# A Winograd-style convolution on one core: ten matmuls over zeros, one more casting load, one more store in halves

## The chip, the core and the metric

The kernel runs on one core of a Trainium2 chip. The core has a matrix engine (TensorE, PE in the profile, with its weight loads as PEld), VectorE (DVE), ScalarE (ACT), GpSimd (POOL) and SyncE (SP), and 16 DMA engines that move data between the device memory and the on-chip memory. The metric is the device time of one execution in microseconds; where several executions were timed, their median.

## The reference

The operation is a 3x3 convolution with a padding of one, over 16 images of 64 channels and 64x64 pixels, to 128 output channels, all in float32:

```python
batch, c_in, h, w, c_out = 16, 64, 64, 64, 128
x_pad = np.pad(x, ((0, 0), (0, 0), (1, 1), (1, 1)), mode='constant')
for kh in range(3):
    for kw in range(3):
        output[b, co] += weight[co, ci, kh, kw] * x_pad[b, ci, kh:kh+h, kw:kw+w]   # over all b, co, ci
```

The input is 16.8 MB, the output 33.6 MB.

## The kernel before, in words

Two images make a pair: 2 x 64 channels fill the 128 partitions. There are eight pairs, p = 0 to 7. In float16, the kernel computes two output rows j and j+1 at a time from three groups of products: U, from the sum of the two input rows in the middle (`ss`) with the weights' middle row G1; A, from single rows (`xs`) with G2-G1 and G0; B, from single rows with G0-G1 and G2. The even output rows are A + U, the odd ones B + U. Each group is a set of matmuls of 64 partitions by up to 512 columns, alternating between the two images of the pair, into two PSUM tiles (tag `acc`, 8 buffers).

Preparation: SP loads the weights (L42), pair 0 as float32 (`x0`, L45), and pairs 1 to 3 as float32 (`xf`, L49), all on one queue. POOL makes an identity and a float16 copy of the weights (L53). PE transposes the nine taps (L85, 18 small matmuls), ACT copies them out (L86), and POOL forms the differences G2-G1 and G0-G1 (L87, L88). POOL then issues `load(4)`: a DMA that reads float32 and writes float16 straight into an `xs` tile (L59). The `xs` pool has five buffers, so loads of pairs 5, 6 and 7 wait until an earlier pair's matmuls are done. Pair 0 is summed by DVE (L68) and cast by ACT (L92) in four pieces.

The main loop runs over the pairs. At its head POOL makes the row sums of the next pair (L68, two pieces) and, from p = 1 on, issues the load of pair p + 4. Then come four blocks of eight row pairs each. In a block PE computes U, ACT copies U out of PSUM (L155), PE computes A and DVE adds (L165), PE computes B and DVE adds (L168). For pairs that came in as float32 (`xf`), ACT also casts a quarter of the next pair twice in each of the blocks 2 and 3 (L160).

Stores: each pair has two output tiles of 2 MB, one per image (`ots`, tag `ot`, eight buffers, which the float32 inputs share). SP stores the first (L97 through `store`), ACT the second; the ACT store is held back until ACT has copied U of the next block (L161). A pair is stored whole after its last block, except pair 7, which is stored in two halves after blocks 1 and 3.

The order of each engine's instructions follows the program where `keep` marks them; the rest is placed by a scheduler, which also puts in the waits.

Of the kernel before, what the change touches and what calls it, by code (L numbers as in the profile page):

```python
# [8 lines left out]
F32 = mybir.dt.float32  # L9
F16 = mybir.dt.float16  # L10
# [3 lines left out]
def kernel(  # L14
# [6 lines left out]
    nc = tc.nc  # L21
    B, CI, H, W = x.shape
    CO = weight.shape[0]
    assert H == 64 and W == 64 and CI == 64 and CO == 128 and B % 2 == 0
    NP = B // 2
    RB = 8

    keep = tc.keep_in_program_order
# [4 lines left out]
    const = ctx.enter_context(tc.tile_pool(name="const", bufs=1))  # L33
    psum = ctx.enter_context(tc.tile_pool(name="psum", bufs=8, space=bass.MemoryType.PSUM))
    xpool = ctx.enter_context(tc.tile_pool(name="xpool", bufs=5))
# [8 lines left out]
    cuts = [(0, 18), (18, 34), (34, 50), (50, 64)]  # L44
    nc.sync.dma_start(x0, x_rows[0:128, :, :])  # L45
    xf = {}
    for p in (1, 2, 3):
        xf[p] = opool.tile([128, H, W], F32, tag="ot", name="xf")
        nc.sync.dma_start(xf[p], x_rows[128 * p : 128 * p + 128, :, :])  # L49
    ident = const.tile([128, 128], F16)  # L50
    make_identity(nc, ident)
    w16 = const.tile([CO, CI * 9], F16)
    keep(nc.gpsimd.tensor_copy(w16, w_raw))  # L53

    xs = {p: xpool.tile([128, H, W], F16, tag="xs", name="xs") for p in range(4)}

    def load(p):
        xs[p] = xpool.tile([128, H, W], F16, tag="xs", name="xs")
        keep(nc.gpsimd.dma_start(xs[p], x_rows[128 * p : 128 * p + 128, :, :]))  # L59
# [3 lines left out]
    def sums(eng, p, src, lo, n):  # L63
        if p not in ss:
            ss[p] = spool.tile([128, H // 2, W], F16, tag="ss", name="ss")
        v = src.rearrange("p (j i) c -> p j i c", i=2)
        keep(
            eng.tensor_add(  # L68
                ss[p][:, lo : lo + n, :], v[:, lo : lo + n, 0, :], v[:, lo : lo + n, 1, :]
            )  # L70
        )
# [5 lines left out]
    def wrow(i):  # L77
        return Wt[:, i, :, :].rearrange("p t c -> p (t c)")

    for kh, g in ((1, G1), (2, G2), (0, G0)):  # L80
        wp = psum.tile([128, 512], F32, tag="acc", name="wp")
        for k in range(3):
            t = 3 * kh + k
            for q in (0, 64):
                nc.tensor.matmul(wp[q : q + 64, k * CO : k * CO + CO], w16[:, t::9], ident)  # L85
        keep(nc.scalar.copy(wrow(g), wp[:, 0 : 3 * CO]))  # L86
    keep(nc.gpsimd.tensor_sub(wrow(G21), wrow(G2), wrow(G1)))  # L87
    keep(nc.gpsimd.tensor_sub(wrow(G01), wrow(G0), wrow(G1)))  # L88
    load(4)
    for n, (lo, hi) in enumerate(cuts):  # L90
        sums(nc.vector, 0, x0, RB * n, RB)
        keep(nc.scalar.copy(xs[0][:, lo:hi, :], x0[:, lo:hi, :]))  # L92
# [3 lines left out]
    def store(eng, p, b2, ot, lo, hi):  # L96
        return eng.dma_start(  # L97
            out_rows[2 * p + b2, :, lo:hi, :],
            ot.rearrange("p j i c -> p (j i) c")[:, lo:hi, :],
        )  # L100

    for p in range(NP):
        if p + 1 < NP:
            for lo in (0, 16):
                sums(nc.gpsimd, p + 1, xf.get(p + 1, xs[p + 1]), lo, 16)
        if p > 0 and p + 4 < NP:
            load(p + 4)
        ots = [
            opool.tile([128, H // 2, 2, W], F32, tag="ot", name="ot") for _ in range(2)
        ]  # L110
        for blk in range(4):
            j0 = blk * RB

            def group(wi_rows):

                tiles = [
                    psum.tile([128, RB, W], F32, tag="acc", name="acc") for _ in range(2)
                ]
                n = 3 * len(wi_rows)
                i = 0  # L120
                for wi, off in wi_rows:
                    for kw in (1, 0, 2):
                        c_lo, c_hi = max(0, 1 - kw), min(W, W + 1 - kw)
                        for b2 in range(2):
                            p0 = 64 * b2
                            lo, hi = j0, j0 + RB
                            if off is None:
                                rhs = ss[p][p0 : p0 + 64, lo:hi, c_lo + kw - 1 : c_hi + kw - 1]
                            else:
                                while 2 * lo + off < 0:  # L130
                                    lo += 1
                                while 2 * (hi - 1) + off > H - 1:
                                    hi -= 1
                                first = 2 * lo + off
                                last = 2 * (hi - 1) + off
                                rhs = xs[p][
                                    p0 : p0 + 64,
                                    first : last + 1 : 2,
                                    c_lo + kw - 1 : c_hi + kw - 1,
                                ]  # L140
                            nc.tensor.matmul(  # L141
                                tiles[b2][:, lo - j0 : hi - j0, c_lo:c_hi],
                                Wt[p0 : p0 + 64, wi, kw, :],
                                rhs,
                                start=i == 0,
                                stop=i == n - 1,
                            )
                        i += 1
                return tiles

            U = group([(G1, None)])
            us = []
            for b2 in range(2):
                ut = upool.tile([128, RB, W], F32, tag="ut", name="ut")
                keep(nc.scalar.copy(ut, U[b2]))  # L155
                us.append(ut)
            if p + 1 in xf:
                q = p + 1
                for lo in {2: (0, 16), 3: (32, 48)}.get(blk, ()):
                    keep(nc.scalar.copy(xs[q][:, lo : lo + 16, :], xf[q][:, lo : lo + 16, :]))  # L160
            while held:  # L161
                keep(store(nc.scalar, *held.pop(0)))
            A = group([(G21, 1), (G0, -1)])
            for b2 in range(2):
                nc.vector.tensor_add(ots[b2][:, j0 : j0 + RB, 0, :], A[b2], us[b2])  # L165
            Bt = group([(G01, 0), (G2, 2)])
            for b2 in range(2):
                nc.vector.tensor_add(ots[b2][:, j0 : j0 + RB, 1, :], Bt[b2], us[b2])  # L168
            parts = {3: (0, 64)} if p < NP - 1 else {1: (0, 32), 3: (32, 64)}
            if blk in parts:  # L170
                lo, hi = parts[blk]
                store(nc.sync, p, 0, ots[0], lo, hi)
                held.append((p, 1, ots[1], lo, hi))
# [32 lines left out]
```

## Time and profile before

| | before |
|---|---|
| time, median of 3 runs | 127.69 us (126.99 to 127.93) |
| the profiled execution's own time | 128.37 us |
| its span, first to last instruction | 126.6 us |
| PE busy | 105.8 us (84%) |
| DVE busy | 82.7 us (65%) |
| ACT busy | 52.0 us (41%) |
| POOL busy | 36.2 us (29%) |
| DMA packets | 46.57 MB written, mean 368 GB/s |
| device memory | 17.07 MB read, 33.55 MB written |

A line of the groups reads: source line, engine, operation, output <- inputs, shapes, count, then busy time, mean ns of one, and idle time before it with what ended it. A row of the stretches reads: from and to, length, busy us and count of PE, PEld, DVE, ACT and POOL, then the granted TensorE clock, the share of the 16 DMA engines' time in packets, and GB/s. Packets are counted in the stretch in which they start, so a share can pass 1. A casting load counts with the bytes that it writes, half of those that it reads. The issue of a DMA stands under the queue's name (SPq, ACTq, POOLq) or, for POOL, among its instructions; it says when the transfer was asked for, not when it moved.

### The profile page before, as it was taken

How to read it: one execution, taken by the hardware profiler on the slowest of the kernel's cores; microseconds unless marked ns; L12 is line 12 of the kernel's file. 1: busy time of each engine (PE TensorE's matmuls, PEld its weight loads, DVE VectorE, ACT ScalarE, POOL GpSimd, SP SyncE). 2: the span in 40 equal slices, each digit the busy share in tenths (PEclk: the TensorE clock that was granted, in tenths of full speed). 3: DMA queues.
4: the chain of work that ended last, by engine and by line, in shares of the span. 5: the costliest groups of instructions: out<-in, count | busy, mean ns of one | idle time of the engine just before them, and what ended most of it. 6: DMA issues, size and time to landing. Idle time of an engine off the chain costs nothing.

```text
span 126.6 us, 2416 instructions
## 1 busy us (share of the span) xinstructions
PE 105.8 (84%) x978; PEld 57.2 (45%) x978; DVE 82.7 (65%) x132; ACT 52.0 (41%) x84; POOL 36.2 (29%) x27
## 2 busy tenths in 40 slices
PE   0409999999999999999999999999999999990000
PEld 0304455555555555555555555555555555540000
DVE  0025777787778777877777778777877787774000
ACT  4329429933993399333333333333333333330000
POOL 2360093197996000940066000750000000000000
PEclk9999999999999999999999999999999999999855
DMA  6899999999999999999999999999999979999970
GB/s 171 352 456 394 295 306 363 430 440 430 391 324 290 362 396 334 347 321 375 368 352 362 303 409 419 430 419 425 435 430 425 399 316 425 414 438 414 417 324 21
DMA packets 3898, 46.57 MB, mean 368 GB/s; under 512 B 432, under 2 KB 432, under 8 KB 560
## 3 DMA queue, kind: packets, MB, share of 16 engines
q1 hardware_dynamic: 2016, 25.46, 48.2%
q10 hardware_dynamic: 1296, 16.78, 31.5%
q0 software_dynamic: 576, 4.19, 15.8%
q8 instruction: 7, 0.11, 0.3%
q14 instruction: 3, 0.02, 0.0%
HBM read 17.07 MB, written 33.55 MB: 400 GB/s over the span
## 4 chain that ended last, share of the span: by engine, by line
PE 82%; DMA 6%; DVE 2%; issue 1%; DVEq 0%; SPq 0%
PE acc L141 82%; DMA x<-in_x_dram 6%; DVE ot L165 1%; DVE ss L68 1%; DVE ot L168 0%; DVEq L201 0%; SPq L42 0%; DVEq L165 0%
## 5 line engine op out<-in xcount | busy, mean ns | idle before, releaser
L141 PE MATMUL acc<-xs,Wt 64*128 64x504 f16 (+3 forms) x768 | 88.8, 377 | 0.0
L141 PEld LDWEIGHTS <-Wt 64*128 64x128 f16 x960 | 56.1, 95 | 52.0 <-issue 6.0
L165 DVE TENSOR_TENSOR ot<-acc,ut 128x512 f32<-128x512 f32 x64 | 41.2, 686 | 23.8 <-PE acc L141 21.5
L155 ACT COPY ut<-acc 128x512 f32<-128x512 f32 x64 | 34.4, 589 | 54.3 <-issue 34.3
L168 DVE TENSOR_TENSOR ot<-acc,ut 128x512 f32<-128x512 f32 x64 | 41.1, 684 | 0.0
L141 PE MATMUL acc<-ss,Wt 64*128 64x504 f16 (+1 forms) x192 | 27.2, 384 | 3.9 <-DVE ss L68 3.9
L68 POOL TENSOR_TENSOR ss<-xs 128x1024 f16<-128x1024 f16 x8 | 16.8, 2127 | 20.4 <-DMA xs<-in_x_dram 20.4
L68 POOL TENSOR_TENSOR ss<-xf 128x1024 f16<-128x1024 f32 x6 | 14.0, 2355 | 12.5 <-DMA xf<-in_x_dram 12.5
L160 ACT CAST xs<-xf 128x1024 f16<-128x1024 f32 x12 | 12.0, 1057 | 0.0
L68 DVE TENSOR_TENSOR ss<-x 128x512 f16<-128x512 f32 x4 | 2.5, 685 | 8.8 <-DMA x<-in_x_dram 8.8
L59 POOL DMA_DIRECT2D xs<-in_x_dram x4 | 2.4, 601 | 10.4 <-ACT xs L160 10.4
L92 ACT CAST xs<-x 128x1024 f16<-128x1024 f32 (+2 forms) x4 | 3.9, 1042 | 2.6 <-DMA x<-in_x_dram 2.6
L85 PE MATMUL wp<-ident,w 128*64 128x128 f16 x18 | 1.3, 328 | 4.3 <-POOL w L53 4.3
L85 PEld LDWEIGHTS <-w 128*64 128x64 f16 x18 | 1.1, 209 | 4.3 <-POOL w L53 4.3
L86 ACT CAST Wt<-wp 128x384 f16<-128x384 f32 x3 | 1.2, 487 | 3.0 <-PE wp L85 3.0
L86 ACT ACT_TABLE_LOAD x1 | 1.3, 1283 | 0.7 <-PEq L190 0.7
L87 POOL TENSOR_TENSOR Wt<-Wt 128x384 f16<-128x384 f16 x1 | 0.9, 910 | 1.7 <-ACT Wt L86 1.7
L53 POOL CAST w<-w_raw 128x576 f16<-128x576 f32 x1 | 0.7, 664 | 2.3 <-DMA w_raw<-in_weight_dram 2.3
L88 POOL TENSOR_TENSOR Wt<-Wt 128x384 f16<-128x384 f16 x1 | 0.9, 910 | 0.0
masks.py:199 POOL TENSOR_SCALAR_AFFINE_SELECT ident<-ident 128x128 f16<-128x128 f16 x1 | 0.3, 294 | 0.1
masks.py:197 POOL MEMSET ident<- 128x128 f16 x1 | 0.2, 205 | 0.3 <-POOLq L190 0.3
L190 POOL MEMSET const-float32-0.0<- 128x1 f32 x1 | 0.1, 99 | 0.2 <-issue 0.2
(3 smaller groups left out, 0.3 us busy)
## 6 DMA issues: line engine op xcount, KB each, us to landing
out_dram<-ot SPq DMA_DIRECT2D x7, 2048.0 KB, 20.0
out_dram<-ot ACTq DMA_DIRECT2D x7, 2048.0 KB, 19.6
xf<-in_x_dram SPq DMA_DIRECT2D x3, 2048.0 KB, 22.6
xs<-in_x_dram POOLq DMA_DIRECT2D x4, 1024.0 KB, 24.2
x<-in_x_dram SPq DMA_DIRECT2D x1, 2048.0 KB, 7.6
out_dram<-ot SPq DMA_DIRECT2D x2, 1024.0 KB, 11.3
out_dram<-ot ACTq DMA_DIRECT2D x2, 1024.0 KB, 11.2
w_raw<-in_weight_dram SPq DMA_DIRECT2D x1, 288.0 KB, 2.8
```

Of the source, the lines that this page charges most:

```text
L59: keep(nc.gpsimd.dma_start(xs[p], x_rows[128 * p : 128 * p + 128, :, :]))
L68: eng.tensor_add(ss[p][:, lo : lo + n, :], v[:, lo : lo + n, 0, :], v[:, lo : lo + n, 1, :])
L85: nc.tensor.matmul(wp[q : q + 64, k * CO : k * CO + CO], w16[:, t::9], ident)
L86: keep(nc.scalar.copy(wrow(g), wp[:, 0 : 3 * CO]))
L87: keep(nc.gpsimd.tensor_sub(wrow(G21), wrow(G2), wrow(G1)))
L88: keep(nc.gpsimd.tensor_sub(wrow(G01), wrow(G0), wrow(G1)))
L92: keep(nc.scalar.copy(xs[0][:, lo:hi, :], x0[:, lo:hi, :]))
L141: nc.tensor.matmul(tiles[b2][:, lo - j0 : hi - j0, c_lo:c_hi], Wt[p0 : p0 + 64, wi, kw, :], rhs, start=i == 0, stop=i == n - 1,)
L155: keep(nc.scalar.copy(ut, U[b2]))
L160: keep(nc.scalar.copy(xs[q][:, lo : lo + 16, :], xf[q][:, lo : lo + 16, :]))
L165: nc.vector.tensor_add(ots[b2][:, j0 : j0 + RB, 0, :], A[b2], us[b2])
L168: nc.vector.tensor_add(ots[b2][:, j0 : j0 + RB, 1, :], Bt[b2], us[b2])
```

## The change

Three things are changed.

1. A tile of zeros is set by DVE, and ten matmuls over it (128 x 512, into a PSUM tile that nobody reads) are put on PE behind the transposes. The transposes get `keep`, so that PE's order is transposes, zeros, convolution.
2. Pair 3 is no longer loaded as float32 by SP and cast by ACT. It comes by a casting load on POOL, issued just before that of pair 4. `xs` is preset for three pairs instead of four, the fourth buffer going to `load(3)`. One buffer of the tag `ot` is no longer taken by an input.
3. Pair 6 is stored in halves, as pair 7 is.

```diff
-    for p in (1, 2, 3):
+    for p in (1, 2):
         xf[p] = opool.tile([128, H, W], F32, tag="ot", name="xf")
         nc.sync.dma_start(xf[p], x_rows[128 * p : 128 * p + 128, :, :])
+    zeros = const.tile([128, 512], F16)
+    keep(nc.vector.memset(zeros, 0.0))
+    warm = psum.tile([128, 512], F32, tag="acc", name="warm")
+
+    def spin(n):
+        for _ in range(n):
+            keep(nc.tensor.matmul(warm, zeros[:, 0:128], zeros))
+
...
-    xs = {p: xpool.tile([128, H, W], F16, tag="xs", name="xs") for p in range(4)}
+    xs = {p: xpool.tile([128, H, W], F16, tag="xs", name="xs") for p in range(3)}
...
             for q in (0, 64):
-                nc.tensor.matmul(wp[q : q + 64, k * CO : k * CO + CO], w16[:, t::9], ident)
+                keep(nc.tensor.matmul(wp[q : q + 64, k * CO : k * CO + CO], w16[:, t::9], ident))
         keep(nc.scalar.copy(wrow(g), wp[:, 0 : 3 * CO]))
+    spin(10)
     keep(nc.gpsimd.tensor_sub(wrow(G21), wrow(G2), wrow(G1)))
     keep(nc.gpsimd.tensor_sub(wrow(G01), wrow(G0), wrow(G1)))
-    load(4)
+    for p in (3, 4):
+        load(p)
...
-            parts = {3: (0, 64)} if p < NP - 1 else {1: (0, 32), 3: (32, 64)}
+            parts = {3: (0, 64)} if p < NP - 2 else {1: (0, 32), 3: (32, 64)}
```

In text and code pairs are numbered from 0: the fourth pair is p = 3, the seventh p = 6.

## The prediction

> **What bounds the kernel now.** I read the chain that ended last first, then the DMA queues, then the last stretches. The chain names PE; the question is whether that is the whole story.
>
> ```profile
> PE 82%; DMA 6%; DVE 2%; issue 1%; DVEq 0%; SPq 0%
> ...
> 9.55 103.26 PE acc L141 x948
> ...
> 114.78 0.33 SPq L97 DMA_DIRECT2D out_dram<-ot  x1
> 115.38 0.34 ACTq L97 DMA_DIRECT2D out_dram<-ot  x1
> ...
> SPq L201 <- DMA out_dram<-ot: 10.2, 5, 4.2
> ```
>
> PE works without a break from 9.55 to 112.81 us, but the span is 126.6. The last two stores are issued at 114.78 and 115.38, and SP then waits 10.2 us for stores at the kernel's end (L201). Those stores are 1 MB each; two of them at 426 GB/s take 4.9 us. The rest of the wait is a backlog: the end is set by DMA. The queues (packets, MB, share of the span on 16 engines) say how full it is:
>
> ```profile
> q1 hardware_dynamic: 2016, 25.46, 48.2%
> q10 hardware_dynamic: 1296, 16.78, 31.5%
> q0 software_dynamic: 576, 4.19, 15.8%
> q8 instruction: 7, 0.11, 0.3%
> ```
>
> They add up to 95.8%, 121.3 of 126.6 us. What is missing is seen in the stretches (the last two columns are DMA share and GB/s written):
>
> ```profile
> 80.00:98.00 18.00, 18.00 (x172) 9.75 (x168) 13.79 (x23) 5.90 (x12) 4.12 (x2) 1.00 1.01 428
> 98.00:100.00 2.00, 2.00 (x22) 1.04 (x18) 1.33 (x3) 1.07 (x2) 0.00 (x0) 1.00 1.02 434
> 100.00:102.00 2.00, 2.00 (x22) 1.16 (x20) 1.94 (x4) 0.10 (x1) 0.00 (x0) 1.00 0.67 279
> 102.00:104.00 2.00, 2.00 (x24) 1.09 (x20) 1.42 (x3) 0.97 (x2) 0.00 (x0) 1.00 0.75 320
> 104.00:106.00 2.00, 2.00 (x22) 1.10 (x20) 1.66 (x3) 0.93 (x2) 0.00 (x0) 1.00 1.14 483
> 106.00:120.00 14.00, 8.00 (x76) 4.08 (x71) 7.51 (x12) 2.29 (x5) 0.00 (x0) 0.97 0.99 419
> 120.00:122.00 2.00, 0.00 (x0) 0.00 (x0) 0.00 (x0) 0.00 (x0) 0.00 (x0) 0.50 1.01 426
> 122.00:124.00 2.00, 0.00 (x0) 0.00 (x0) 0.00 (x0) 0.00 (x0) 0.00 (x0) 0.50 0.32 135
> 124.00:126.00 2.00, 0.00 (x0) 0.00 (x0) 0.00 (x0) 0.00 (x0) 0.00 (x0) 0.50 0.04 16
> ```
>
> There are two thin places. One is a hole at 100 to 104 us: pair 5's stores have run out on most engines, and pair 6's are issued only at 101.97 (SP) and 102.58 (ACT). The other is a tail after 122 where only a few of the 16 engines still move data. The tail decides. Each transfer leaves 16 completion marks in the trace, which I read as one per DMA engine (sorted, us):
>
> ```
> pair 5, second store: 101.15 101.27 101.28 101.40 101.44 101.53 101.54 101.60 101.78 102.62 102.85 102.99 103.78 104.25 104.83 106.24
> last store:           122.76 122.78 122.79 122.79 122.80 122.81 122.81 122.82 122.83 122.84 122.88 123.10 123.58 123.78 124.73 125.61
> ```
>
> The slowest engine finished pair 5 at 106.24, long after pair 6's stores were there: it **never saw the hole**. From 106.24 to 125.61 it moved its sixteenth of the last 8.39 MB, 0.524 MB in 19.37 us = 27.1 GB/s, and 16 times that is 433, the full rate of the rows above. So the kernel ends when one late engine has done its share, and that engine is full from about 2 us on.
>
> **The change, part by part.**
>
> *Zeros and ten matmuls.* The memset of 128x512 f16 on DVE has no row; POOL's 128x128 memset took 0.205 us, so 0.2 to 0.8 us. DVE is idle until 8.80: cost nothing. The conv matmuls go in pairs of 64 rows; a spin fills 128 rows, so it should cost one pair's pace:
>
> ```profile
> 11.63 0.18 PEld L141 LDWEIGHTS <-Wt 64*128 64x128 f16 x2 [0.25 <-issue]
> 12.06 0.18 PEld L141 LDWEIGHTS <-Wt 64*128 64x128 f16 x2 [0.25 <-issue]
> 12.43 0.18 PEld L141 LDWEIGHTS <-Wt 64*128 64x128 f16 x2 [0.20 <-issue]
> 12.81 0.17 PEld L141 LDWEIGHTS <-Wt 64*128 64x128 f16 x2 [0.20 <-issue]
> 13.18 2.75 PEld L141 LDWEIGHTS <-Wt 64*128 64x128 f16 x26 [0.20 <-issue]
> ```
>
> A pair takes 0.43 us at first, 0.38 at the turn and 0.21 from 13.18 on, 3.6 us after PE began at 9.55; this is half pace, though the clock column reads 1.00 there. Nine pairs took 3.63 us and would take 1.9 at 0.21, so at most 1.7 us are to be had. The transposes end at 5.62 (4.31 + 1.31), so ten spins end between 7.7 and 9.9. The first conv matmul waits for DVE until 9.55: at worst 0.4 us late. PE then ends between 1.7 us earlier and 0.4 later. Neither moves the end: the last two stores are 4.9 us of work on the slowest engine, which so reaches them near 120.7, while they are issued by 115.4 plus 0.8 (from issue to rising rate at 101.97 to 102.75). PE has some 4 us of slack there. Gain taken: 0. `keep` on the transposes only fixes an order that the trace already shows.
>
> *Pair 3 by a casting load.* SP loses one 0.43 us issue, ACT four casts of 1.06 us, and two sums on POOL fall from 2.36 to 2.13 us: none on the path. POOL gains one issue of 0.57 to 0.70 us behind L88; queued behind it are the load of pair 4 and the sums of pair 1, for which POOL idles 7.23 us until 15.56. Pair 3 is needed near 48 us; a cast load issued at 7.63 landed by 23.05. SP's queue then has no pair 3 ahead of pair 0's stores. What counts is DMA time. Four casting loads took 15.8% = 20.0 us, 5.00 each; stores 31.5% = 39.9 us for 16.78 MB, 4.98 per 2.1 MB. By packets: 624 ns instead of 611, eight per engine, and plain packets beside casts also take 624: 0.1 + 0.1 us. **The unknown is what a cast does to the slowest engine.** Its lag behind the middle of the 16 is by such marks 1.5 us at 24.7, 2.4 at 30.5, 4.5 at 75.7 and 4.4 at 96.4, when the casts are over. Put on the four casts alone, that is 1.1 each. But there are seven instruction packets too (q8, 0.93 us each, one at 21.04 and then every 11 to 15 us), and the first cast load, beside other loads, left no lengthened packets before that one. Bounds: 0 to 1.1 us for the fifth; I take 0.2, nearer to that first stretch, since the added load runs there too. A gain is excluded, since as many bytes are read.
>
> Here the Trainium skill speaks against the change: "DMA: Bandwidth & Descriptors", section "Latency and other measured facts", has two of the 16 engines usually slower, with the descriptor rings of GpSimd's loads as a best guess. The trace has the late engine, not its number; by that rule the whole 1.1 us would fall due and the sum would be +1.45 us.
>
> *Pair 6 in halves.* SP and ACT each issue one store more (0.33 us). SP has only stores. On ACT the held store waits for DVE with the next copies behind it, as the page's waits show seven times now; ACT idles 54 us and PE's chain has no break there. The first halves come 12.8 us (a pair) before pair 7's 108.33, near 95.5 or 1.7 earlier, so the hole is filled. The packets become 8 KB: 309 ns each, 618 for 611, 16 times per engine = 0.1 us, and two more completions. Ten marks of pair 5 come before 102.75, so ten engines have something to gain, up to 1.9 us (the first falls idle at 100.83); the slowest has nothing: 0.
>
> A second rule of that page, section "Bandwidth", asks for large batches and gives a 1 MB load 78% of the peak. The row 120:122, when only 1 MB stores are left, has 426 GB/s; by the rule each of the four halves would take an estimated 0.6 us more (1.05 MB at 341 instead of 425 GB/s).
>
> **Sum.** 0.1 + 0.1 + 0.1 + 0.05 (completions) + 0.2 = +0.55 us on the span: 127.15. The profiled execution took 128.37, 1.77 around its span; it lies 0.68 above the median 127.69. Relative to the median: 128.2.
>
> **Rivals.**
> *The hole was the end's cause* (faster). If what I call one late engine is not one, but the work is passed on, the end follows the mean. The deficit is 0.94 us by GB/s (149 + 108 - 55, times 2 us, over 428) and up to 1.9 by the idle engines: 125.9 to 126.9 after the 0.15 of packets and completions, 126.4 in the middle. For it: ten engines did idle. Against it: the 19.37 us.
> *The fifth cast delays the late engine like the four before* (slower): 0.35 + 1.1 = +1.45 us, 129.1. It passes 1% from 0.93 us of added lag. For it: the lag grows from 20 to 77 us and not after. Against: the instruction packets, and the stretch of the new load.
> *The warm-up doesn't take*: zeros leave the pace at 0.43. PE ends at 113.2 at worst, inside its slack: 128.2 as well, no case of its own in time.
>
> **Chances.** Forecast: 0.52. Late engine made later: 0.26, all over 1% slower. Hole: 0.22, of which 0.13 over 1% faster and 0.09 within. Within 1% (126.4 to 129.0, about what a measurement of this kernel can tell from no change) that makes 0.61. The range takes in most of the hole's case and, above, 129.1 with 0.4 for a cast that costs more beside pair 0's stores than the average: 126.2 to 129.5.
>
> **What would show it.** Pairs at 0.21 us from the first conv matmul, PE's end near 111; no hole at 100 to 104; most completion marks of the last store near 121; its last mark still at 125 to 126.5. The lag of the last mark against the middle should grow from 2.8 to over 4 us, as the others get earlier. The prediction is wrong if the last mark comes with the others, or if the late engine's lag grows by a microsecond by 80 us.

## The result, and the profile after

The changed kernel takes 126.75 us (median of 22 runs, 126.31 to 127.87) against 127.94 us before (22 runs, 126.82 to 129.93, on the same chips): a ratio of 0.9928 with an interval of 0.9906 to 0.9949. It is faster by 0.7%, about 0.9 us. The ratios, here and below, take only the runs within 1.5% of the fastest of their kernel, the medians take all runs, so one doesn't follow from the other (by the medians the gain is 1.2 us). The forecast was 128.2 us, a little slower than before. The measured time lies in the range and in the bound of 1%, but the sign was wrong. The runs spread over 1.6 us after and over 3.1 us before: the one profile that the prediction was built on, 128.37 us, stood well above the median of its own kernel.

The page of the changed kernel, its queues (packets, MB, share of 16 engines):

```profile
q1 hardware_dynamic: 2016, 23.36, 44.6%
q10 hardware_dynamic: 1440, 16.78, 31.6%
q0 software_dynamic: 720, 5.24, 20.9%
q8 instruction: 7, 0.11, 0.3%
```

The chain that ended last (start, length, what):

```profile
5.64 3.89 PE warm L56 x10
9.53 101.53 PE acc L151 x919
```

The queues' shares add up to 97.4% of 125.0 us, 121.8 us; before it was 121.3. So the DMA engines are as loaded as before and idle less. PE ends at 111.06 instead of 112.81 us, as the zeros cost 3.89 us in a gap that was there. The weight loads show the pace (start, length; each line one spin or a group):

```profile
8.11 0.15 PEld L56 LDWEIGHTS <-zeros 128*128 128x128 f16 x1 [0.28 <-issue]
8.54 0.15 PEld L56 LDWEIGHTS <-zeros 128*128 128x128 f16 x1 [0.28 <-issue]
8.94 0.10 PEld L56 LDWEIGHTS <-zeros 128*128 128x128 f16 x1 [0.25 <-issue]
9.46 0.59 PEld L151 LDWEIGHTS <-Wt 64*128 64x128 f16 x8 [0.42 <-issue]
```

Spins go at 0.43 us until about 8.9; the trace's clock record has the full clock from 8.90 us on, before the first convolution matmul. In the kernel before it starts at 13.27. (The clock column of the stretches reads 1.00 ahead of that first entry, which is why it told nothing.)

The stretches of the changed kernel (the last two columns are DMA share and GB/s written):

```profile
24.00:26.00 2.00, 2.00 (x22) 1.05 (x20) 1.40 (x3) 0.42 (x1) 0.59 (x1) 1.00 1.14 205
26.00:28.00 2.00, 2.00 (x22) 1.06 (x20) 1.27 (x3) 1.07 (x2) 2.00 (x2) 1.00 0.96 143
...
100.00:102.00 2.00, 2.00 (x22) 1.03 (x20) 1.40 (x3) 1.07 (x2) 0.00 (x0) 1.00 1.00 418
102.00:104.00 2.00, 2.00 (x22) 1.08 (x20) 1.94 (x4) 0.64 (x2) 0.00 (x0) 1.00 0.98 414
...
120.00:122.00 2.00, 0.00 (x0) 0.00 (x0) 0.00 (x0) 0.00 (x0) 0.00 (x0) 0.50 0.86 365
122.00:124.00 2.00, 0.00 (x0) 0.00 (x0) 0.00 (x0) 0.00 (x0) 0.00 (x0) 0.50 0.21 86
```

The hole at 100 to 104 us is gone. New is a weak stretch at 24 to 28, where the kernel before has this row:

```profile
26.00:28.00 2.00, 2.00 (x23) 1.06 (x19) 1.70 (x3) 0.13 (x1) 2.00 (x2) 1.00 1.05 426
```

The engines count as busy, but move less. Almost only casting loads run there, so twice the written bytes count, and even then 143 is 286 GB/s. Of the casting loads' packets, which took 624 ns elsewhere, 24 of the 25 that start at 26 to 28 us took 0.7 to 1.56 us; I call this a spell. The completion marks of the changed kernel's last two stores show that the last engine is no longer 2.8 us behind the middle of its store, but 1.4:

```
last store on SP:  120.89 121.45 121.52 121.53 121.54 121.83 121.89 122.32 122.64 123.03 123.12 123.14 123.29 123.31 123.32 123.96
last store on ACT: 121.51 121.75 121.82 121.85 121.87 122.15 122.19 122.63 122.94 123.32 123.33 123.34 123.44 123.48 123.48 124.15
```

In these two executions the last mark went from 125.61 to 124.15 us, while the middle of the last store stayed (122.82 and 122.78). The question is which part made the most loaded engine earlier, and whether it is the same in other executions.

### The profile page after: what moved, and what is told of

Its sections match the earlier page's. It is cut to its first block, busy times and chain, and to the rows that moved or that the text cites. A ratio compares the mean times of both kernels' runs of the same rounds, so it can differ in the third digit from the quotient of the medians.

```text
span 125.0 us, 2436 instructions
## 1 busy us (share of the span) xinstructions
PE 108.1 (86%) x988; PEld 56.7 (45%) x988; DVE 82.8 (66%) x133; ACT 48.2 (39%) x80; POOL 36.4 (29%) x28
## 4 chain that ended last, share of the span: by engine, by line
PE 85%; DMA 2%; DVE 1%; issue 1%; POOL 1%; DVEq 0%
PE acc L151 81%; PE warm L56 3%; DMA w_raw<-in_weight_dram 2%; PE wp L93 1%; DVE ot L175 1%; POOL w L61 1%; DVEq L211 0%; DVE ot L178 0%; DVEq L175 0%
## 5 line engine op out<-in xcount | busy, mean ns | idle before, releaser
L151 PE MATMUL acc<-xs,Wt 64*128 64x504 f16 (+3 forms) x768 | 93.1, 373 | 0.0
L151 PEld LDWEIGHTS <-Wt 64*128 64x128 f16 x960 | 54.3, 94 | 48.6 <-issue 0.8
L151 PE MATMUL acc<-ss,Wt 64*128 64x504 f16 (+1 forms) x192 | 31.8, 377 | 0.0
L76 POOL TENSOR_TENSOR ss<-xs 128x1024 f16<-128x1024 f16 x10 | 21.0, 2126 | 21.7 <-DMA xs<-in_x_dram 11.1
L76 POOL TENSOR_TENSOR ss<-xf 128x1024 f16<-128x1024 f32 x4 | 9.4, 2364 | 11.8 <-DMA xf<-in_x_dram 11.8
L170 ACT CAST xs<-xf 128x1024 f16<-128x1024 f32 x8 | 8.0, 1058 | 0.0
L67 POOL DMA_DIRECT2D xs<-in_x_dram x5 | 2.9, 587 | 9.3 <-PE acc L151 9.3
L56 PE MATMUL warm<-zeros 128*128 128x512 f16 x10 | 4.0, 574 | 0.0
L56 PEld LDWEIGHTS <-zeros 128*128 128x128 f16 x10 | 1.3, 137 | 2.3 <-issue 2.2
## 6 DMA issues: line engine op xcount, KB each, us to landing
out_dram<-ot SPq DMA_DIRECT2D x4, 1024.0 KB, 13.2
out_dram<-ot ACTq DMA_DIRECT2D x4, 1024.0 KB, 12.8
```

The costliest lines, as they stand in the source:

```text
L56: keep(nc.tensor.matmul(warm, zeros[:, 0:128], zeros))
L76: eng.tensor_add(ss[p][:, lo : lo + n, :], v[:, lo : lo + n, 0, :], v[:, lo : lo + n, 1, :])
L151: nc.tensor.matmul(tiles[b2][:, lo - j0 : hi - j0, c_lo:c_hi], Wt[p0 : p0 + 64, wi, kw, :], rhs, start=i == 0, stop=i == n - 1,)
```

## Experiments

Each was timed in 12 runs (the one with eight short spins in 6) beside the kernel before on the same chip. For reading them side by side I use one table, made from the DMA records of each profiled execution: how many MB the 16 engines are behind a steady 0.4275 MB per us that starts at 2.5 us (a casting load counted by what it reads, instruction packets left out). 0.43 MB is 1 us of all engines. "Clock" is the first full-clock entry of the clock record.

| kernel | median us | ratio to before (interval) | clock full from | first store issued | behind at 24 | at 48 | at 100 | at 104 us | last mark |
|---|---|---|---|---|---|---|---|---|---|
| before, first profile | 127.69 | | 13.27 | 25.13 | 0.07 | 0.16 | 0.35 | 0.81 | 125.61 |
| before, again | 127.25 | 0.9968 (0.9914 to 1.0022) | 14.94 | 26.06 | 0.07 | 0.68 | 0.78 | 1.15 | 125.18 |
| whole change | 126.75 | 0.9928 (0.9906 to 0.9949) | 8.90 | 23.42 | -0.03 | 0.50 | 0.51 | 0.55 | 124.15 |
| halves alone | 127.75 | 1.0042 (0.9999 to 1.0084) | 15.03 | 25.97 | 0.03 | 0.68 | 0.76 | 0.77 | 125.26 |
| cast alone | 127.23 | 0.9996 (0.9959 to 1.0033) | 12.34 | 24.72 | 0.03 | 0.24 | 0.33 | 0.61 | 123.94 |
| zeros alone | 126.58 | 0.9945 (0.9911 to 0.9978) | 8.58 | 23.80 | 0.02 | 0.47 | 0.49 | 0.53 | 123.90 |
| zeros and halves | 127.13 | 0.9963 (0.9935 to 0.9991) | 10.05 | 23.82 | 0.01 | 0.53 | 0.53 | 0.57 | 124.22 |
| zeros and cast | 126.78 | 0.9951 (0.9920 to 0.9983) | 7.74 | 23.45 | 0.06 | 0.46 | 0.49 | 0.54 | 124.09 |
| cast and halves | 126.77 | 0.9977 (0.9941 to 1.0014) | 14.50 | 26.33 | 0.07 | 0.87 | 0.93 | 0.93 | 125.16 |
| zeros, 8 full spins late | 128.04 | 1.0041 (1.0015 to 1.0067) | 8.91 | 23.90 | 0.09 | 0.45 | 0.48 | 1.05 | 125.63 |
| zeros, 8 short spins late | 126.57 | 0.9889 (0.9845 to 0.9932) | 7.63 | 23.48 | 0.03 | 0.48 | 0.50 | 0.56 | 123.74 |
| zeros, pair 6's stores later | 126.67 | 0.9957 (0.9926 to 0.9988) | 10.12 | 23.78 | 0.01 | 0.49 | 0.51 | 0.81 | 124.00 |
| zeros, pair 0's stores later | 127.51 | 0.9996 (0.9958 to 1.0034) | 8.68 | 24.99 | 0.05 | 0.35 | 0.47 | 0.52 | 124.24 |
| whole, pair 0's stores later | 127.64 | 0.9994 (0.9954 to 1.0034) | 9.47 | 25.07 | 0.05 | 0.11 | 0.22 | 0.25 | 123.47 |
| pair 0 in halves alone | 127.58 | 1.0015 (0.9978 to 1.0052) | 14.68 | 19.35 | 0.12 | 0.32 | 0.40 | 1.15 | 125.36 |
| whole, pair 0 in halves | 127.34 | 0.9970 (0.9936 to 1.0003) | 8.12 | 17.71 | 0.18 | 0.44 | 0.46 | 0.49 | 124.04 |

A profile is one execution; the medians are of twelve runs (three in the first row, 22 for the whole change, six with eight short spins). The kernel before was profiled twice, and the two rows differ by 0.5 MB at 48 us.

### The kernel before, once more

No edit.

> The kernel before, unchanged, for a second profile. Theory A (a property of the program): the last store's 16 completion marks look as they did, fifteen within 2 us of the middle and the last one 2.8 us behind it, and the late mark is 4 to 5 us behind the middle from 75 us on. Theory B (a draw of the run): the late mark's lag differs by more than 1 us from one execution to the next, and the time with it. Time within 0.5% either way.

As to the lag, theory B held: here the last mark lies 1.5 us behind the middle of its store, not 2.8. In this execution the clock rose at 14.94 instead of 13.27 us, so more convolution matmuls went at half pace. This execution's weight loads around the rise:

```profile
14.23 0.17 PEld L141 LDWEIGHTS <-Wt 64*128 64x128 f16 x2 [0.25 <-issue]
14.65 0.17 PEld L141 LDWEIGHTS <-Wt 64*128 64x128 f16 x2 [0.25 <-issue]
15.01 0.97 PEld L141 LDWEIGHTS <-Wt 64*128 64x128 f16 x10 [0.18 <-issue]
```

PE's chain ended at 113.73 against 112.81. In the six profiles without zeros the clock rose at 12.34 to 15.03 us: a draw over 2.7 us, half of which PE loses.

Every run has its span and its mean granted clock on record, and this tells whether the time goes with that draw. In all 16 profiles the full clock lasts 102.40, 105.81 or 109.23 us, which is 30, 31 or 32 times 3.413. The mean counts the time ahead of the rise as full, so with the span it gives the moment of the fall and, but for a multiple of 3.413 us, that of the rise (worked out so for the 16 profiled runs, it meets the profile's own to within 0.13 us). Taken to lie between 12.0 and 15.4 us, it splits 134 timed executions of this kernel: the 39 with a rise before 12.75 have a median of 126.9 us, and 22 of them lie under 127; the 37 with a rise after 14.25 have 128.0, and none lies under 127. So the clock's draw moves the time, by about 1 us, but not alone: the 39 reach up to 128.2.

The early loss is a draw too, and comes as a spell at 34 to 44 us that the first profile hardly had. First the rows of the second profile, then those of the first:

```profile
34.00:36.00 2.00, 2.00 (x22) 1.05 (x18) 2.00 (x4) 1.72 (x3) 1.70 (x3) 1.00 0.93 270
42.00:44.00 2.00, 2.00 (x22) 1.09 (x20) 1.27 (x3) 1.03 (x2) 0.00 (x0) 1.00 0.95 258
```

```profile
34.00:36.00 2.00, 2.00 (x22) 1.07 (x20) 1.30 (x3) 1.72 (x4) 1.98 (x3) 1.00 1.01 352
42.00:44.00 2.00, 2.00 (x22) 1.04 (x18) 1.65 (x3) 0.11 (x1) 0.00 (x0) 1.00 0.99 348
```

The two executions end within 0.43 us of each other by different ways: the first has the middle of its last store at 122.82 and one engine 2.79 us behind, the second the middle at 123.73 and 1.45. The late engine of the prediction was real, but how late it is belongs to the execution, not to the program.

### One part of the change at a time

```diff
-            parts = {3: (0, 64)} if p < NP - 1 else {1: (0, 32), 3: (32, 64)}
+            parts = {3: (0, 64)} if p < NP - 2 else {1: (0, 32), 3: (32, 64)}
```

> Pair 6 in halves alone. Theory A (the late engine sets the end): the hole at 100 to 104 us is gone, the time is within 0.3 us of before, since the late engine never saw the hole. Theory C (the hole is the end's cause): 0.9 to 1.6 us faster.

The hole is gone (0.76 behind at 100 us, 0.77 at 104) and the time isn't better: 1.0042, with an interval that just touches 1. Theory C's 0.9 to 1.6 us faster is out, which speaks against the hole as the end's cause by itself. Theory A's 0.3 us holds by the medians (127.75 against 127.62 for the kernel before beside it); the ratio's middle is 0.5 us slower, and whether the halves cost something isn't settled.

```diff
-    for p in (1, 2, 3):
+    for p in (1, 2):
...
-    load(4)
+    for p in (3, 4):
+        load(p)
```

> Pair 3 by a casting load alone. Theory A with a lag that the casts make: 0.2 to 1.5 us slower. Theory A with a lag that the float32 load of pair 3 beside pair 0's stores makes: 0.5 to 1.5 us faster, and the late mark at 75 to 96 us less than 3 us behind the middle. Theory C: within 0.3 us.

0.9996: the casting load costs and brings nothing that 12 runs can tell. Neither of theory A's two forms got its size. The last mark lies 1.4 us behind its middle in this profile, with an early rise of the clock at 12.34 us; with one profile the two can't be parted.

```diff
+    zeros = const.tile([128, 512], F16)
+    keep(nc.vector.memset(zeros, 0.0))
+    warm = psum.tile([128, 512], F32, tag="acc", name="warm")
...
+    spin(10)
```

> The ten matmuls over zeros alone. PE's end is near 111.1 instead of 112.8 us. Theory A: the time is within 0.3 us, since PE has about 4 us of slack against the late engine. Theory C: the hole shrinks by what PE gains, 1.7 us, and the time falls by 0.9 to 1.6 us, as much as by the halves.

0.9945: the zeros alone make three quarters of the whole change's gain, and their interval takes in all of it. The 0.3 us that theory A allowed were passed (0.7 us at the ratio's middle). PE ended at 111.44 and the hole was gone, as theory C said; but theory C had also promised this to the halves, which didn't get it.

### Pairs of parts

Each leaves out one part of the whole change.

> Zeros and halves, pair 3 still as float32. The zeros alone leave no hole, so both theories H and E expect the time of the zeros alone, 0.4 to 0.8% under before; if the halves cost something of their own (alone they were at 1.004), 0.1 to 0.3% faster only.

> The whole change without the halves. Theories H and E: PE is early, no hole, 0.4 to 0.8% faster than before, the same as the whole change. If the halves are what the whole change has over the zeros, less than that.

> The whole change without the ten matmuls. PE's clock rises between 12 and 15.2 us, after the first convolution matmul. Theory H: no hole whatever PE does, so 0.4 to 0.8% faster than before. Theory E: the early loss stays a draw, time within 0.4% of before.

With zeros the ratios are 0.9963 and 0.9951, intervals below 1; without them 0.9977, an interval that takes in 1. The five kernels with zeros and no later delay, the whole change among them, look alike in the table: full clock by 10.05 us, first store at 23.4 to 23.8 us, 0.46 to 0.53 MB behind at 48 us, next to nothing lost after. Those without zeros scatter from 0.16 to 0.87 MB at 48 us. For cast and halves, theory H's figure (0.4 to 0.8% faster) is neither reached nor excluded. Its twelve runs fall into two groups, seven at 126.4 to 126.9 us and five at 127.7 to 128.2, and its profile (127.82 us) is of the second: without the zeros this kernel can be as fast as the whole change, but not in every run.

### The hole put back: eight more spins late

```diff
+        if p == 5:
+            spin(8, psum.tile([128, 512], F32, tag="acc", name="warm2"))
```

> The ten matmuls over zeros, and eight more ahead of pair 5 (about 1.7 us at 0.21 each), so that pairs 5 to 7 come as late as in the kernel before while all earlier stores come early. Theory H (an early PE helps because pair 6's stores then meet no hole): the hole at 100 to 104 us is back, and the 0.5% of the ten matmuls alone are lost, time within 0.3% of before. Theory E (it helps by what happens before 45 us: when the first stores meet the loads): 0.4 to 0.8% faster than before, as with the ten alone.

The gain is lost and more: 1.0041. The eight spins in PE's chain (start, length), and then the stretches of this kernel, which show the hole:

```profile
74.51 1.83 PE warm L56 x8
```

```profile
100.00:102.00 2.00, 2.00 (x22) 0.98 (x20) 1.27 (x3) 0.70 (x2) 0.00 (x0) 1.00 0.88 369
102.00:104.00 2.00, 2.00 (x24) 0.90 (x21) 1.44 (x3) 1.07 (x2) 0.00 (x0) 1.00 0.52 221
```

That looked like theory H. But the run brought an eighth instruction packet of 16 KB (at 115.93 us), and it made all of pairs 5 to 7 late. Two more runs look at these separately.

### The hole put back: only pair 6's stores later

ACT copies an idle tile twice and touches pair 6's first output tile before SP and ACT may store the pair. PE's instructions stay as they were.

```diff
+            while late:
+                for _ in range(2):
+                    keep(nc.scalar.copy(pad, pad))
+                o = late[0][2]
+                keep(nc.scalar.copy(o[:, 0, 0, 0:8], o[:, 0, 0, 0:8]))
+                keep(store(nc.sync, *late.pop(0)))
             while held:
...
+                if p == 6:
+                    late.append((p, 0, ots[0], lo, hi))
```

> The ten matmuls alone, but ACT does two idle copies and a touch of pair 6's first output tile before SP and ACT may store pair 6: these two stores come 1.5 to 2 us later, PE and its instruction count stay. Theory H (the zeros help because pair 6's stores meet no hole): the hole at 100 to 104 us is back and the time is 0.5 to 1.2 us over the ten matmuls alone, which puts it within 0.4% of before. Theory L (they help because less is left for the most loaded engine by 80 us, and what the eight extra matmuls cost was an eighth instruction packet): hole, but less than 0.4 us over the ten matmuls alone.

SP's store moved from 100.64 to 102.91 us, ACT's from 101.24 to 102.17. The stretches of this kernel:

```profile
100.00:102.00 2.00, 2.00 (x24) 0.92 (x20) 1.42 (x3) 1.46 (x3) 0.00 (x0) 1.00 0.86 360
102.00:104.00 2.00, 2.00 (x22) 0.92 (x20) 2.00 (x4) 1.19 (x4) 0.00 (x0) 1.00 0.83 344
```

A hole of 0.30 MB, 0.7 us of all engines, and the time stays: 126.67 us, ratio 0.9957. As to the hole, theory L held. Pair 6's stores were issued at 102.17 and 102.91, and about half of the marks of pair 5's stores come before 103 us: the hole fell to engines that were ahead. The last mark is at 124.00, as with the zeros alone.

### The same instructions without the delay

```diff
-            spin(8, psum.tile([128, 512], F32, tag="acc", name="warm2"))
+            for _ in range(8):
+                keep(nc.tensor.matmul(warm2[:, 0:8], zeros[:, 0:128], zeros[:, 0:8]))
```

> The ten matmuls, and ahead of pair 5 eight matmuls of 8 columns instead of 512: as many instructions as in the run with eight full ones, but some 0.5 us of PE instead of 1.7. If that run was slow by its eighth instruction packet near 116 us, this one has that packet too and is 0.7 to 1.3 us over the ten matmuls alone. If it was slow by PE's 1.7 us, this one is within 0.5 us of the ten alone.

The eight short matmuls in PE's chain:

```profile
74.10 0.29 PE warm L120 x8
```

The eighth instruction packet came (113.96 us), pair 6's first store went out at 100.91 us instead of 102.87 (0.4 us of that is a later start of the convolution in the profile with full spins), and the time is 126.57 instead of 128.04. So the packet by itself costs nothing. 1.5 us more of PE, from pair 5 on, cost 1.5 us, though the last stores still went out at 115.7 and 116.3 us; this goes directly against the prediction's "some 4 us of slack". Whether PE's lateness costs this by itself, or only together with the packet, isn't shown: a late PE from pair 5 on without an eighth packet wasn't run. In the run with full spins the marks of a store at 114 us lie within 0.8 us of each other; of the next, behind that packet at 115.93, the last mark is 2.0 us behind the middle.

### When the first stores start

The delay of pair 6's stores, moved to pair 0: the same edit with `p == 0`, on the zeros alone and on the whole change.

> The same delay on pair 0's stores instead, so that the first stores come at 25 us as in the kernel before while PE's clock is up from the start. Theory S (the spell of lengthened packets at 25 to 28 us comes when the first stores meet the loads at that moment): no spell or another place for it, the loss by 44 us under 0.2 MB instead of 0.42, up to 0.5 us faster than the ten matmuls alone. Theory P (it goes with PE's pace): spell unchanged, time unchanged within 0.3 us.

> The whole change with the same delay on pair 0's stores. Theory S: up to 0.5 us faster than the whole change, some 1% under before. Theory P: as the whole change, 0.5 to 0.9% under before.

The stretches of the zeros alone, and then of the same with pair 0's stores held back by 0.6 us (ACT) and 1.9 us (SP):

```profile
26.00:28.00 2.00, 2.00 (x22) 1.09 (x20) 1.48 (x3) 1.07 (x2) 2.00 (x2) 1.00 0.95 262
```

```profile
26.00:28.00 2.00, 2.00 (x22) 1.04 (x19) 1.27 (x3) 1.07 (x2) 2.00 (x2) 1.00 1.00 418
```

The spell at 25 to 28 us went, as theory S said; on the zeros alone a smaller one came at 40 to 48 us (0.24 MB), on the whole change none of note. The time did not follow: 0.9996 and 0.9994, the gain gone in both. PE kept its pace (its chain is 101.56 us long with and without the delay on the zeros alone), so it isn't PE that lost it. Nor is it the added instructions: the same ones at pair 6 cost nothing (0.9957). What came back is the scatter: 126.78 to 129.78 us for the zeros, 126.20 to 131.01 for the whole change, where the kernels themselves have 126.19 to 127.56 and 126.31 to 127.87. The profiled execution of the second is the earliest of all, 124.4 us of span with 0.25 MB behind at 104 us; four others of the same kernel took 2.1 to 4.8 us more. In the profiles, first stores at 24.7 to 26.3 us thus go with a draw (0.06 to 0.80 MB lost from 24 to 48 us), those at 23.4 to 23.9 with a middling loss that hardly varies (0.36 to 0.53 MB). The second, on average, is better.

### First stores much earlier

```diff
-            parts = {3: (0, 64)} if p < NP - 1 else {1: (0, 32), 3: (32, 64)}
+            parts = {3: (0, 64)} if 0 < p < NP - 1 else {1: (0, 32), 3: (32, 64)}
```

On the kernel before; on the whole change the same with `0 < p < NP - 2`.

> The kernel before with pair 0 stored in halves: the first stores are issued near 19 us instead of 25, the others as before, and PE's clock stays a draw. Theory F (what the ten matmuls bring is that the first stores are issued before 24.5 us): 0.4 to 0.8% faster than before and a spread of the runs under 0.5 us. Theory K (it needs PE at full pace from the start, whatever the stores do): within 0.4% of before, spread 0.7 us or more.

> The whole change with pair 0 stored in halves, first stores near 17 us. Theory F: as the whole change or up to 0.5 us faster, if a still earlier start loses less than the 0.4 MB of the spell at 25 to 28 us. Theory K: as the whole change within 0.3 us.

Theory F fell: with first stores at 19.35 us and PE's clock left to its draw, 1.0015; with the whole change, 0.9970, not better than the change itself. Early first stores are not enough. Theory K fits the first of the two, but not the runs with held-back stores, where PE is at full pace from the start and the gain is gone. In the first of the two PE was late (clock at 14.68, pair 7's last store issued at 116.4 us), and 0.75 MB went in the hole.

## Why the prediction was wrong

**What held.** The end is set by DMA: in every profile the last mark comes 0.9 to 1.3 us before the end of the span, while PE's chain ends 12.8 and 13.1 us ahead of that mark in the two kernels. The halves alone bring nothing although they fill the hole (1.0042), as the sum had it. No run shows the 0.05 us for completions by itself. The casting load's 0.4 us in all can't be told from nothing (0.9996). The spins ended at 9.53, inside the predicted 7.7 to 9.9, PE ended near 111, pairs go at 0.21 us from the start, and the hole is gone. The rival that the fifth cast makes the late engine 1.1 us later is out: alone it is at 0.9996, at most 0.4 us slower by its interval. The guess that the Trainium skill has on it ("DMA: Bandwidth & Descriptors", section "Latency and other measured facts": two engines usually slower, with the descriptor rings of GpSimd's loads as a best guess) gets no support here, since one such load more cost nothing that 12 runs can tell; which engine is late, the traces don't name. The other signs failed: most marks of the last store were to come near 121, its last at 125 to 126.5 with a lag of over 4 us; the middle is at 122.78, the last mark at 124.15, and the lag 1.4.

**The step that failed** is this one: "Neither moves the end: [...] PE has some 4 us of slack there. Gain taken: 0." The slack was worked out at one place, the last two stores, and from one execution. The runs show two things in its place. First, PE's pace sets the moment of every store, the first ones too. Held back to 25 us with PE at full pace, pair 0's stores cost the whole gain (0.9996 instead of 0.9945). Second, there is no such slack late either: 1.5 us of PE from pair 5 on cost 1.5 us (128.04 against 126.57 at the same number of instructions, the eighth instruction packet in both), though pair 6's stores alone could be later for nothing (126.67).

**The second failing** lies ahead of that step: the late engine was taken as a property of the program, with a lag of 4.5 us from 75 us on. It differs from one execution to the next: at the end of the 16 profiles the last mark lies 0.9 to 2.8 us behind the middle of its store. The moment at which the clock rises differs too, and the time of the kernel before goes with it in part (126.9 us for early rises, 128.0 for late ones). The prediction saw the rise at 13.2 us and priced it as a fixed 1.7 us of PE; that the rise is a draw was not considered, and therefore not that ten matmuls take this draw away. The Trainium skill says so: "TensorE: Matmul & The Clock Gate", Part 1, describes a free-running window and a transition that moves by half a microsecond from run to run. The rows agree on the draw and show a wider one: 12.34 to 15.03 us in the six profiles without zeros, always by 10.12 in the ten with them.

**What the sum should have had.** A term for the zeros of -0.7 us (0.9945 of 127.7), and 0 for the other two parts. Within the intervals the three single ratios, multiplied (0.998), don't contradict the whole change's 0.9928, but don't explain it closely either.

**What stays open.** Why packets lengthen in spells at 25 to 44 us, and why their place hangs on the moment of the first stores, was not settled. In a spell many packets of one queue at a time take 0.7 to 1.6 us instead of 0.6: the casting loads at 24 to 28 us in the changed kernel, SP's queue at 25 to 28 with the zeros alone, and in the second profile of the kernel before ACT's stores at 34 to 40 and then the casting loads at 40 to 44. Nor why late stores of all of pairs 5 to 7 cost 1.5 us where those of pair 6 cost nothing. The hole was larger there (0.57 MB against 0.30). One reading, not tested: a hole levels the engines (in the run with eight full spins thirteen of the last 16 marks lie within 0.13 us), and whatever one engine loses afterwards, such as by the eighth instruction packet, then stands on top; there the last mark was 1.9 us behind the level.

## What to carry to other kernels

When the end is a DMA backlog, an engine off the chain still decides when transfers meet each other, so its slack can't be read at the last transfer alone; a delay put in by hand at the first and at the last transfers shows both. Before arguing from the lag of one engine, profile the same kernel twice: here the very late engine and the missing spell of the first profile were that execution's own. And a warm-up that fills an idle gap takes one random start-up cost out of every run. It doesn't make the runs alike by itself: zeros and cast still lay at 126.22 to 129.91 us.

## What the runs showed of the hardware

- The moment of the full clock lay between 12.34 and 15.03 us in kernels whose convolution starts at 9.5 to 10.7 us, and between 7.63 and 10.12 us with ten spins from 5.6 us on (16 profiles). The full clock then lasted 102.40 us (two profiles), 105.81 (nine) or 109.23 (five).
- A store issued to busy DMA engines begins late: pair 0's ACT store, issued at 24.02 us, had its first packet at 28.38; pair 6's, into the hole of the kernel before, saw the rate rise 0.8 us after issue.
- 16 more PE instructions (988 matmuls and 988 weight loads became 996 of each) brought an eighth 16 KB instruction packet near the end (113.96 us), without a cost in the median (126.57 against 126.58).
